# A two-layer diffusion backbone on one core: operand build in single splits, a deferred activation, and a down projection whose second half runs in reverse

## The chip, the cores and the metric

The kernel runs on one core of a Trainium2 chip. The core has TensorE (PE, matrix products; PEld is its loading of stationary operands), VectorE (DVE), ScalarE (ACT), GpSimd (POOL) and SyncE (SP, which here only issues DMAs). Each engine works through its own list of instructions in order. The metric is the device time of one execution in microseconds (us), lower is better.

## The reference

Two layers over 1024 latent tokens of width 1024 and, in the first layer, 256 context tokens. Layer 0 mixes tokens by a gated MLP in chunks of 128, layer 1 by windowed attention; each is followed by the same channel mixer, which is what most of the change touches:

```python
def conv_ffn(h, w_up, conv_w, conv_b, w_down):
    a, b = jnp.split(h @ w_up, 2, axis=-1)           # w_up (1024, 5632), so a and b have 2816 columns
    ap = jnp.pad(a, ((0, 0), (1, 1), (0, 0)))
    a = ap[:, :-2] * conv_w[0] + ap[:, 1:-1] * conv_w[1] + ap[:, 2:] * conv_w[2] + conv_b
    return (jax.nn.gelu(a) * b) @ w_down             # w_down (2816, 1024)
...
    for i in range(DEPTH):                           # 2
        mod_lat = silu(c) @ ada_w[i] + ada_b[i]      # six rows: shift, scale, gate, twice; the same for ctx
        h = modulate(rms_norm(x, norm_g[i, 0]), sh1, sc1)
        y, yc = chunk_mlp(...) if i == 0 else window_attention(...)
        x = x + g1 * rms_norm(y, norm_g[i, 1])
        h = modulate(rms_norm(x, norm_g[i, 2]), sh2, sc2)
        x = x + g2 * rms_norm(conv_ffn(h, f_w_up[i], ...), norm_g[i, 3])
```

## The kernel before

Every operand of a product is split into a high part (an ACT cast, `wh`, `ah` or `cmb`) and the rest (a DVE subtract, `wl`, `al` or `cmb`), so that each product is three matmuls (`mm3`). The weights come by SP's DMAs into three `raw` buffers, which all loads of the kernel share, and are split from there (`split_into`).

**Order.** The code is written as generators: `step` takes one piece of a side job (a weight's split, a column of the operand build) between products. A scheduler then orders each engine's list by its own estimates; the lists are fixed before the kernel runs. The lines that time belongs to are hidden behind one helper (L50), so the rows name tiles.

**Layer 0 up.** First 22 context blocks (`up_ctx`, 48 matmuls of 256 columns each, with weights of 128 columns of a and of b) with `combine(0)` and `combine(1)` as side jobs in 44 steps: they load the modulated tokens (`xT`) and build seven split operands (`COMBOS`, tiles `cmb`) for Strassen's scheme. Then 22 Strassen blocks (`up`), each 7 products of 12 matmuls of 512 columns; their weight sums t1 to t4 are built by `weights` while the block before runs. X, Y and Z are PSUM tiles (`psB`): the copy of b1 reads Y after the second product, and a PSUM tile must be read before a product overwrites it. `conv_gate` does the convolution (two DVE adds), gelu (ACT), the product with b (DVE) and the store to `actd`; it runs beside the next block's products.

**Layer 0 down.** Two halves of 512 output columns. Each loads all 22 activation blocks (`act_hl`, tiles `ah` and `al`) and the weights of its half, two blocks a load; eight PSUM banks (four in two `psA` tiles, four in `psB`) gather eight token tiles. The last blocks of a half run bank by bank, and `finish` reads each bank, by a square on ACT (`junk`) and a gated copy on DVE (`y`). As a side job the sums of the next layer's ada weights run on DVE (`dacc`, 32 loads: two sets of eight with two sums each, two sets with one).

**Layer 1** has the same without context: attention ends in an output product (`last_o`), then a few plain blocks beside `combine(0)`, 22 Strassen blocks (five of them half ones, `g1`, 256 columns), and the down projection. `flip` (transposes of a normed tile, with eight modulates from PSUM to SBUF) stands between mixers and channel mixers.

Of the kernel before, what the change touches and what calls it, by code (L numbers as in the profile page):

```python
# [10 lines left out]
F32 = mybir.dt.float32  # L11
# [4 lines left out]
P = 128  # L16
# [16 lines left out]
def hybrid_kernel(  # L33
# [151 lines left out]

    def ada_sums(l, m, streams, accs):
        for k in range(KD):
            raw = t_raw()
            Q.dma_start(raw, ada_w[l, k * P:(k + 1) * P, m * D:(m + 1) * D])
            for s, acc in zip(streams, accs):  # L190
                cc = ccols[:, 8 * s + k:8 * s + k + 1]
                if k == 0:
                    V.tensor_scalar(out=acc, in0=raw, scalar1=cc, scalar2=None, op0=ALU.mult)
                else:
                    V.scalar_tensor_tensor(out=acc, in0=raw, scalar=cc, in1=acc, op0=ALU.mult, op1=ALU.add)
            yield
# [91 lines left out]
    def flip(stage, t, xn, wide=False, mod=None):  # L288
        xt = t_row(shape=(P, KD, P))
        pw = psA((P, KD, P)) if wide else None  # L290
        pq = [pw[:, 4 * q:4 * q + 4, :] if wide else psB((P, 4, P)) for q in range(2)]
        for k in range(KD):
            T.transpose(out=pq[k // 4][:, k % 4, :], in_=xn[:, k * P:(k + 1) * P], identity=ident)
        for k in range(KD if mod else 0):
            gg, sh = (mod_cols(mod[0], m, 0 if t < 8 else 1)[:, k:k + 1] for m in (mod[1] + 1, mod[1]))
            S.activation(xt[:, k, :], pq[k // 4][:, k % 4, :], AF.Identity, bias=sh, scale=gg)
        for q in range(0 if mod else 2):
            S.copy(xt[:, 4 * q:4 * q + 4, :], pq[q])
        S.dma_start(xT[stage][:, :, t * P:(t + 1) * P], xt)
        return xt  # L300
# [631 lines left out]
    def weights(l, f, out, plain):  # L932
# [24 lines left out]
        t1, t3, t2, t4 = t13[:, 0:512], t13[:, 512:1024], t24[:, 0:512], t24[:, 512:1024]  # L957
        G.tensor_tensor(out=t1, in0=b12, in1=b11, op=ALU.subtract)
        V.tensor_sub(t2, b22, t1)
        G.tensor_tensor(out=t3, in0=b22, in1=b12, op=ALU.subtract)  # L960
        V.tensor_sub(t4, b21, t2)
        yield
        pair((b11, ("b11",)), (t2, ("t2",)))
        yield
# [7 lines left out]
    def lat_ffn(l, stage, n0, halos, gate, between, steady, ctx=None, after=None):  # L972
# [18 lines left out]
        def combine(g):  # L991
            for c in range(2):
# [12 lines left out]
                if ctx is not None:  # L1005
# [7 lines left out]
                    yield  # L1013
                put("a11", a11)
                put("a12", a12)
                if n0 and g == 0:
                    split_into([A21[c][:, z] for z in range(2)], a21)
                put("a22", a22)
                yield
                G.tensor_tensor(out=s1, in0=a21, in1=a22, op=ALU.add)  # L1020
                V.tensor_tensor(out=s2, in0=s1, in1=a11, op=ALU.subtract)
                put("s2", s2)
                G.tensor_tensor(out=s3, in0=a11, in1=a21, op=ALU.subtract)
                put("s1", s1)
                yield
                put("s3", s3)
                V.tensor_tensor(out=s4, in0=a12, in1=s2, op=ALU.subtract)
                put("s4", s4)
                yield
# [10 lines left out]
        def conv_gate(f, a, N, b, where):  # L1040
# [4 lines left out]
                                   op0=ALU.mult, op1=ALU.add)  # L1045
            S.activation(c, c, AF.Gelu_apprx_tanh)
            cv = c.rearrange("p (h n) -> p h n", n=256) if len(b.shape) == 3 else c
            V.tensor_tensor(out=cv, in0=cv, in1=b, op=ALU.mult)
            Q.dma_start(actd[f, :, where:where + N], c)

# [57 lines left out]
        def up(f, groups, nxt):  # L1108
# [31 lines left out]
            S.copy(b1, wide(Y[:, 0:n]))  # L1140
            V.tensor_tensor(out=b1, in0=b1, in1=wide(s1), op=ALU.add)
            product(Z, "s1", "t1", True)
            s5 = t_s()[:, 0:n]
# [42 lines left out]
        for (f, how), nxt in zip(jobs, jobs[1:] + [None]):  # L1186
# [7 lines left out]
            step(steady)  # L1194

        open_pool("down%d" % l)
        pool = stage_pool["pool"]
        ks = list(range(n0, NF)) + list(range(n0))
        ys, sums = {}, []
        if ctx is not None:  # L1200
            extra = chain(*[sums_of(pool, sums, 1, m, streams)
# [4 lines left out]
        def act_hl(k, own):  # L1206
            raw = t_raw()
            Q.dma_start(raw, actd[k, :, 0:SEQ])
            hl = [t_w("w" + z) if own else pool.tile([P, 1024], F32R, name=nm("a" + z), tag="a" + z, bufs=7)
                  for z in "hl"]  # L1210
# [9 lines left out]

        parts = {}
        for h in range(2):
            pair = [psA() for _ in range(2)]
            banks = [pair[i // 2][:, i % 2, :] for i in range(4)] + [psB() for _ in range(4)]
            ws, hls = {}, {}

            def step_(n, i):
                (ah, al), (wh, wl) = hls[n], ws[n]
                tk = slice(i * P, (i + 1) * P)
                mm3(banks[i], ah[:, tk], al[:, tk], wh, wl, n == 0, n == NF - 1)  # L1230

            def fetch(n):
                hls[n] = act_hl(ks[n], h == 0 and n < 2)
                if n % 2 == 0:
# [8 lines left out]

            nk = NF - (2, 6)[h]
            for n in range(nk):
# [31 lines left out]
    def sums_of(pool, sums, l, m, streams):  # L1277
        accs = [pool.tile([P, 1024], F32, name=nm("dacc"), tag="dacc%d%d" % (m, s), bufs=1) for s in streams]
        yield from ada_sums(l, m, streams, accs)
        sums.append((m, streams, accs))  # L1280
# [566 lines left out]
```

## Time and profile before

| | |
|---|---|
| median of 3 runs | 2988.23 us (2986.74 to 2988.72) |
| profiled execution | 2990.52 us, span 2988.7 us, mean granted clock 0.988 |
| busy: TensorE | 2851.6 us (95% of the span), weight loads 2411.1 |
| busy: DVE, ACT, POOL | 2023.8 (68%), 1380.9 (46%), 675.6 (23%) |
| DMA | 493.32 MB, mean 165 GB/s |

In the tables of stretches the granted clock is a mean over the stretch: TensorE's clock has two levels, 2.4 GHz (1.00) and 1.2 GHz (0.5). Waits are named by the engine and tile that waited, and what released it. The stages by time: gated MLP to 780, context blocks to about 925, Strassen blocks of layer 0 to 1381, its down projection to 1640, context down projection and attention to 2250, the start of layer 1's channel mixer to 2340, its Strassen blocks to 2735, its down projection to the end.

### The profile page before, as it was taken

What the parts mean: (1) busy time and instruction counts of PE and PEld (TensorE: products, weight loads), DVE (VectorE), ACT (ScalarE), POOL (GpSimd) and SP (SyncE); (2) the same over time, 40 slices, a digit from 0 to 9 for tenths busy, and PEclk for the clock granted to TensorE, in tenths of its full rate; (3) what the DMA queues carried; (4) which work ended last, traced back from release to release, by engine and by line L of the source; (5) the groups of instructions that cost most, each with busy time, mean ns of one, the idle gap of its engine ahead of it and who ended that gap; (6) DMA issues with size and microseconds to landing.
All of it is one profiled execution on the core that took longest, in us unless ns stands there. A gap on an engine that the chain in (4) does not pass through costs nothing. (4 is left out here: it accounts for less than half of the span.)

```text
span 2988.7 us, 40216 instructions
## 1 busy us (share of the span) xinstructions
PE 2851.6 (95%) x14834; PEld 2411.1 (81%) x14834; DVE 2023.8 (68%) x3008; ACT 1380.9 (46%) x2341; POOL 675.6 (23%) x1019
## 2 busy tenths in 40 slices
PE   7999999999889999999999999999998999999999
PEld 5799888998789777887778777788887878888887
DVE  6457674756586778777663659897776877776333
ACT  4332242422675444543333534787886444444331
POOL 1151120720311112220002114565453211110000
PEclk9999999999999999999999999999998999999999
DMA  8764355532675323445775875347576333235542
GB/s 265 231 182 140 124 192 181 170 97 71 201 216 157 108 92 113 160 158 177 229 233 178 267 257 173 105 150 238 170 243 211 103 121 103 82 95 174 189 148 99
DMA packets 403750, 493.32 MB, mean 165 GB/s; under 512 B 17633, under 2 KB 297057, under 8 KB 403553
## 3 DMA queue, kind: packets, MB, share of 16 engines
q1 hardware_dynamic: 347137, 427.56, 44.8%
q10 hardware_dynamic: 55264, 58.99, 5.7%
q0 software_dynamic: 1152, 4.19, 0.4%
q8 instruction: 117, 1.92, 0.3%
q14 instruction: 80, 0.66, 0.1%
HBM read 394.21 MB, written 96.47 MB: 164 GB/s over the span
## 5 line engine op out<-in xcount | busy, mean ns | idle before, releaser
L50 PE MATMUL psB<-cmb,wh 128*128 128x512 f32 (+2 forms) x2584 | 758.6, 378 | 18.7 <-ACT row L50 16.3
L50 ACT CAST wh<-raw 128x1024 fp32r<-128x1024 f32 (+1 forms) x388 | 345.9, 903 | 491.3 <-PE psB L50 202.9
L50 PEld LDWEIGHTS psB<-cmb,wh 128*128 128x128 f32 x2584 | 469.5, 188 | 124.6 <-ACT row L50 28.8
L50 DVE TENSOR_TENSOR wl<-raw,wh 128x1024 fp32r<-128x1024 f32 (+1 forms) x388 | 404.3, 1053 | 155.2 <-ACT wh L50 154.2
L50 PE MATMUL psB<-cmb,wl 128*128 128x512 f32 (+2 forms) x1292 | 486.4, 376 | 0.0
L50 PE MATMUL psB<-wh,big 128*128 128x512 f32 x864 | 288.7, 401 | 2.1 <-ACT big L50 1.3
L50 PEld LDWEIGHTS psB<-cmb,wl 128*128 128x128 f32 x1292 | 242.8, 188 | 48.2
L50 POOL TENSOR_SCALAR sm<-sm 128x1 f32<-128x1 f32 (+1 forms) x76 | 36.7, 482 | 882.4 <-ACT junk L50 329.8
L50 DVE TENSOR_TENSOR al<-raw,ah 128x1024 fp32r<-128x1024 f32 x84 | 102.8, 1225 | 176.8 <-ACT ah L50 176.7
L50 POOL TENSOR_TENSOR row<-raw,raw 128x512 f32<-128x512 f32 x44 | 72.4, 1646 | 641.1 <-DMA raw<-in_f_w_up_dram 533.5
L50 PE MATMUL psB<-wh,act 128*128 128x512 f32 x640 | 202.9, 395 | 1.6 <-DVE tmp L50 1.6
L50 ACT CAST ah<-raw 128x1024 fp32r<-128x1024 f32 x84 | 87.9, 1048 | 251.0 <-DMA raw<-actd 126.4
L50 PEld LDWEIGHTS psB<-wh,big 128*128 128x128 f32 x864 | 163.7, 190 | 41.7 <-ACT big L50 2.4
L50 PE MATMUL psA<-big,wh 128*128 128x320 f32 x1024 | 194.5, 312 | 2.8 <-ACT wh L50 1.7
L50 ACT CAST wh<-row 128x512 fp32r<-128x512 f32 (+1 forms) x132 | 100.9, 765 | 150.3 <-PE psB L50 66.3
L50 PE MATMUL psB<-wl,big 128*128 128x512 f32 x432 | 168.3, 399 | 0.0
L50 DVE SCALAR_TENSOR_TENSOR row<-row,cwcols,row 128x1024 f32<-128x1024 f32 (+2 forms) x142 | 146.6, 1034 | 31.7 <-issue 16.8
L50 PEld LDWEIGHTS psA<-big,wh 128*128 128x128 f32 x1024 | 160.8, 189 | 3.8 <-ACT wh L50 2.2
L50 POOL TENSOR_SCALAR row<-row,sm,sm 128x128 f32<-128x128 f32 x160 | 121.1, 771 | 148.6 <-DMA row<-vscr 147.9
L50 DVE TENSOR_TENSOR row<-raw,row 128x512 f32<-128x512 f32 (+2 forms) x101 | 117.5, 1163 | 46.9 <-POOL row L50 46.7
L50 PE MATMUL psA<-wh,ah 128*128 128x512 f32 x336 | 133.8, 401 | 14.2 <-ACT wh L50 7.7
L50 PE MATMUL psB<-row,wh 128*128 128x256 f32 x744 | 141.9, 292 | 5.4 <-ACT wh L50 5.2
(263 smaller groups left out, 6248.3 us busy)
## 6 DMA issues: line engine op xcount, KB each, us to landing
raw<-in_f_w_up_dram SPq DMA_DIRECT2D x142, 512.0 KB, 4.8
raw<-in_ada_w_dram SPq DMA_DIRECT2D x96, 512.0 KB, 4.6
raw<-actd SPq DMA_DIRECT2D x93, 512.0 KB, 4.0
raw<-in_a_w_in_dram SPq DMA_DIRECT2D x64, 512.0 KB, 4.7
wh<-woscr SPq DMA_DIRECT2D x48, 512.0 KB, 3.7
raw<-in_f_w_down_dram SPq DMA_DIRECT2D x88, 256.0 KB, 4.1
actd<-row SPq DMA_DIRECT2D x39, 512.0 KB, 2.6
raw<-in_a_w_out_dram SPq DMA_DIRECT2D x35, 512.0 KB, 3.4
```

Source lines behind the costliest of these rows:

```text
L50: ins = fn(*a, **kw)
```

## The change

Five edits. (a) `flip`: the odd ones of the eight modulates go from ACT to DVE. (b) `combine`: one split a step instead of three, s1 and s3 from POOL to DVE; eight or nine steps a column group instead of four or five. (c) `weights`: POOL's t1 and t3 in the first step; DVE's t2, its split, then t4 in the second (before, t2 and t4 in the first). (d) `conv_gate`: gelu, product with b and store are put off (`late`) and issued by `run_late` in the next block, behind the second product's b1 add; half blocks (N < 512) and context blocks do them at once. (e) `down`: the loads of the ada sums have two buffers of their own (`araw`), the second half takes the 22 blocks in reverse and keeps the last five splits of the first (`KEEP`), so it loads 17 blocks of activations instead of 22; in layer 0 the splits have 6 buffers instead of 7, and the last 5 blocks (before 6) run bank by bank.

```diff
     def ada_sums(l, m, streams, accs, space=None):
         for k in range(KD):
-            raw = t_raw()
+            raw = (space or t_raw)()
...
         for k in range(KD if mod else 0):
             gg, sh = (mod_cols(mod[0], m, 0 if t < 8 else 1)[:, k:k + 1] for m in (mod[1] + 1, mod[1]))
-            S.activation(xt[:, k, :], pq[k // 4][:, k % 4, :], AF.Identity, bias=sh, scale=gg)
+            if k % 2:
+                V.tensor_scalar(out=xt[:, k, :], in0=pq[k // 4][:, k % 4, :], scalar1=gg, scalar2=sh,
+                                op0=ALU.mult, op1=ALU.add)
+            else:
+                S.activation(xt[:, k, :], pq[k // 4][:, k % 4, :], AF.Identity, bias=sh, scale=gg)
...
         G.tensor_tensor(out=t1, in0=b12, in1=b11, op=ALU.subtract)
+        G.tensor_tensor(out=t3, in0=b22, in1=b12, op=ALU.subtract)
+        yield
         V.tensor_sub(t2, b22, t1)
-        G.tensor_tensor(out=t3, in0=b22, in1=b12, op=ALU.subtract)
+        pair((b11, ("b11",)), (t2, ("t2",)))
         V.tensor_sub(t4, b21, t2)
-        yield
-        pair((b11, ("b11",)), (t2, ("t2",)))
         yield
...
                 put("a11", a11)
+                yield
                 put("a12", a12)
                 if n0 and g == 0:
                     split_into([A21[c][:, z] for z in range(2)], a21)
+                yield
                 put("a22", a22)
+                V.tensor_tensor(out=s1, in0=a21, in1=a22, op=ALU.add)
                 yield
-                G.tensor_tensor(out=s1, in0=a21, in1=a22, op=ALU.add)
+                put("s1", s1)
                 V.tensor_tensor(out=s2, in0=s1, in1=a11, op=ALU.subtract)
+                yield
                 put("s2", s2)
-                G.tensor_tensor(out=s3, in0=a11, in1=a21, op=ALU.subtract)
-                put("s1", s1)
+                V.tensor_tensor(out=s3, in0=a11, in1=a21, op=ALU.subtract)
                 yield
                 put("s3", s3)
                 V.tensor_tensor(out=s4, in0=a12, in1=s2, op=ALU.subtract)
+                yield
                 put("s4", s4)
...
-            S.activation(c, c, AF.Gelu_apprx_tanh)
-            cv = c.rearrange("p (h n) -> p h n", n=256) if len(b.shape) == 3 else c
-            V.tensor_tensor(out=cv, in0=cv, in1=b, op=ALU.mult)
-            Q.dma_start(actd[f, :, where:where + N], c)
+
+            def rest():
+                S.activation(c, c, AF.Gelu_apprx_tanh)
+                cv = c.rearrange("p (h n) -> p h n", n=256) if len(b.shape) == 3 else c
+                V.tensor_tensor(out=cv, in0=cv, in1=b, op=ALU.mult)
+                Q.dma_start(actd[f, :, where:where + N], c)
+
+            late.append(rest)
+            if len(b.shape) == 3 or N < 512:
+                run_late()
...
             V.tensor_tensor(out=b1, in0=b1, in1=wide(s1), op=ALU.add)
+            run_late()
             product(Z, "s1", "t1", True)
...
         if ctx is not None:
             extra = chain(*[sums_of(pool, sums, 1, m, streams)
                             for m, streams in ((0, (0, 1)), (1, (0, 1)), (3, (0,)), (4, (0,)))])
...
-            hl = [t_w("w" + z) if own else pool.tile([P, 1024], F32R, name=nm("a" + z), tag="a" + z, bufs=7)
+            hl = [t_w("w" + z) if own else pool.tile([P, 1024], F32R, name=nm("a" + z), tag="a" + z, bufs=7 if ctx is None else 6)
...
             def fetch(n):
-                hls[n] = act_hl(ks[n], h == 0 and n < 2)
+                if h == 0 or n >= KEEP:
+                    hls[ks[n]] = act_hl(ks[n], h == 0 and n < 2)
...
-            nk = NF - (2, 6)[h]
+            nk = NF - (2, 6 if ctx is None else 5)[h]
+            if h == 1:
+                ks.reverse()
...
-        yield from ada_sums(l, m, streams, accs)
+        yield from ada_sums(l, m, streams, accs,
+                            lambda: pool.tile([P, 1024], F32, name=nm("araw"), tag="araw", bufs=2))
```

How the lists move at three places (before first, then after; `...` leaves rows out).

DVE in a Strassen block of layer 0. `wl_1480` is the last split of the running block's weights, the SCALAR_TENSOR_TENSOR rows on `row_1481` are the two convolution adds, `row_1489` holds t2 and then t4, `gate` is an ada sum, `row_1491` is b.

```order
L50 TENSOR_TENSOR wl_1480_9633<-row_1468_9511,wh_1479_9632 128x512
L50 SCALAR_TENSOR_TENSOR row_1481_9636<-row_1474_9591,cwcols0_688,row_1481_9636 128x1024
L50 TENSOR_TENSOR row_1489_9655<-raw_1487_9651,row_1488_9654 128x512
L50 SCALAR_TENSOR_TENSOR row_1481_9636<-row_1474_9591,cwcols0_688,row_1481_9636 128x1024
L50 TENSOR_TENSOR row_1489_9655<-raw_1486_9650,row_1489_9655 128x512
L50 SCALAR_TENSOR_TENSOR gate_1354_8777<-raw_1503_9787,ccols_90,gate_1354_8777 128x1024
L50 TENSOR_TENSOR row_1481_9636<-row_1481_9636,row_1470_9542 128x1024
L50 TENSOR_TENSOR row_1491_9686<-row_1491_9686,s_1490_9672 128x2x256
L50 TENSOR_TENSOR wl_1494_9705<-raw_1486_9650,wh_1493_9704 128x512
```

```order
L50 TENSOR_TENSOR wl_1480_9633<-row_1468_9508,wh_1479_9632 128x512
L50 SCALAR_TENSOR_TENSOR row_1481_9636<-row_1474_9591,cwcols0_688,row_1481_9636 128x1024 x2
L50 SCALAR_TENSOR_TENSOR gate_1354_8774<-raw_1503_9784,ccols_90,gate_1354_8774 128x1024
L50 TENSOR_TENSOR row_1481_9636<-row_1481_9636,row_1470_9537 128x1024
L50 TENSOR_TENSOR row_1491_9681<-row_1491_9681,s_1490_9667 128x2x256
L50 TENSOR_TENSOR row_1489_9652<-raw_1487_9648,row_1488_9651 128x512
L50 TENSOR_TENSOR wl_1494_9704<-raw_1486_9647,wh_1493_9703 128x512
L50 TENSOR_TENSOR row_1489_9652<-raw_1486_9647,row_1489_9652 128x512
L50 TENSOR_TENSOR wl_1494_9704<-row_1489_9652,wh_1493_9703 128x512
```

t2 stood between the two adds and t4 behind them; now both adds stand together, and t2 comes behind the product with b and the b1 add, beside the splits of b11 and t2.

ACT at the start of the context blocks. `wh_1091` and `wh_1095` are the casts of the next block's weights, `row_1050` and `row_1041` the flips' modulates, `row_1053`, `row_1055` and `row_972` (each with an `sm`) the squares of norms, `row_1088` a context block's copy.

```order
L50 CAST wh_1048_6782<-raw_1038_6724 128x1024
L50 ACTIVATE row_1050_6786<-psB_1051_6787,modc_83 128x128 x4
L50 ACTIVATE row_1050_6786<-psB_1052_6788,modc_83 128x128 x4
L50 ACTIVATE row_1055_6811,sm_1056_6812<-row_972_6368 128x1024
...
L50 COPY row_1088_6877<-psB_1086_6851 128x256
L50 CAST wh_1091_6885<-raw_1089_6881 128x1024
L50 ACTIVATE row_1053_6806,sm_1093_6889<-row_1044_6755 128x1024
...
L50 ACTIVATE row_972_6368,sm_1094_6895<-row_1054_6809 128x1024
...
L50 CAST wh_1095_6925<-raw_1090_6882 128x1024
```

```order
L50 CAST wh_1048_6782<-raw_1038_6724 128x1024
L50 ACTIVATE row_1041_6731<-psB_1042_6732,modc_83 128x128
L50 ACTIVATE row_1041_6731<-psB_1043_6733,modc_83 128x128
L50 CAST wh_1091_6885<-raw_1089_6881 128x1024
L50 ACTIVATE row_1050_6786<-psB_1051_6787,modc_83 128x128
L50 ACTIVATE row_1041_6731<-psB_1042_6732,modc_83 128x128
L50 ACTIVATE row_1041_6731<-psB_1043_6733,modc_83 128x128
L50 CAST wh_1095_6925<-raw_1090_6882 128x1024
...
L50 ACTIVATE row_1050_6786<-psB_1051_6787,modc_83 128x128
L50 ACTIVATE row_1050_6786<-psB_1052_6788,modc_83 128x128 x2
L50 ACTIVATE row_1055_6811,sm_1056_6812<-row_972_6368 128x1024
...
L50 COPY row_1088_6877<-psB_1086_6851 128x256
L50 ACTIVATE row_1053_6806,sm_1093_6889<-row_1044_6755 128x1024
```

Both casts stood behind the flip and among the squares; now they stand ahead of all three squares and between single modulates, and the flips have half as many modulates here.

DVE at the turn of the halves in layer 0's down projection. `al` is a split of activations, `wl` of weights, `dacc` an ada sum, `y` the read of a bank.

```order
L50 SCALAR_TENSOR_TENSOR dacc_1895_12362<-raw_1970_12728,ccols_90,dacc_1895_12362 128x1024
L50 TENSOR_TENSOR al_1973_12734<-raw_1971_12731,ah_1972_12733 128x1024
L50 SCALAR_TENSOR_TENSOR dacc_1895_12362<-raw_1974_12761,ccols_90,dacc_1895_12362 128x1024
L50 SCALAR_TENSOR_TENSOR dacc_1895_12362<-raw_1975_12764,ccols_90,dacc_1895_12362 128x1024
L50 TENSOR_TENSOR al_1978_12770<-raw_1976_12767,ah_1977_12769 128x1024
L50 TENSOR_TENSOR wl_1981_12777<-raw_1979_12773,wh_1980_12776 128x1024
L50 SCALAR_TENSOR_TENSOR dacc_1895_12362<-raw_1982_12804,ccols_90,dacc_1895_12362 128x1024
L50 TENSOR_TENSOR y_1935_12596<-psA_1806_11819,gate_1354_8777 128x512
L50 TENSOR_TENSOR al_1985_12810<-raw_1983_12807,ah_1984_12809 128x1024
L50 SCALAR_TENSOR_TENSOR dacc_1895_12362<-raw_1986_12837,ccols_90,dacc_1895_12362 128x1024
L50 TENSOR_TENSOR y_1938_12608<-psA_1806_11819,gate_1354_8777 128x512
L50 TENSOR_TENSOR y_1941_12620<-psA_1807_11820,gate_1354_8777 128x512
```

```order
L50 SCALAR_TENSOR_TENSOR dacc_1895_12362<-araw_1974_12813,ccols_90,dacc_1895_12362 128x1024
L50 SCALAR_TENSOR_TENSOR dacc_1895_12362<-araw_1978_12847,ccols_90,dacc_1895_12362 128x1024
L50 TENSOR_TENSOR al_1981_12853<-raw_1979_12850,ah_1980_12852 128x1024
L50 TENSOR_SCALAR dacc_1982_12880<-araw_1983_12881,ccols_90 128x1024
L50 SCALAR_TENSOR_TENSOR dacc_1982_12880<-araw_1984_12884,ccols_90,dacc_1982_12880 128x1024
L50 TENSOR_TENSOR wl_1972_12759<-raw_1970_12755,wh_1971_12758 128x1024
L50 SCALAR_TENSOR_TENSOR dacc_1982_12880<-araw_1991_12924,ccols_90,dacc_1982_12880 128x1024
L50 SCALAR_TENSOR_TENSOR dacc_1982_12880<-araw_1995_12957,ccols_90,dacc_1982_12880 128x1024
L50 SCALAR_TENSOR_TENSOR dacc_1982_12880<-araw_2002_12997,ccols_90,dacc_1982_12880 128x1024
L50 TENSOR_TENSOR wl_1977_12820<-raw_1975_12816,wh_1976_12819 128x1024
L50 TENSOR_TENSOR y_1935_12596<-psA_1806_11819,gate_1354_8774 128x512
L50 SCALAR_TENSOR_TENSOR dacc_1982_12880<-araw_2006_13030,ccols_90,dacc_1982_12880 128x1024
```

The first three `y` stood behind and between splits of the second half's activations; now seven ada sums (five of the last set, `dacc_1982`) and two splits of weights stand ahead of the first, and of activations only `al_1981`.

## Rows read from the trace of the kernel before

**Rows 1.** the page: busy us, share of the span and instructions of each engine

```profile
PE 2851.6 (95%) x14834; PEld 2411.1 (81%) x14834; DVE 2023.8 (68%) x3008; ACT 1380.9 (46%) x2341; POOL 675.6 (23%) x1019
```

**Rows 2.** stretches; us, busy us of PE, PEld, DVE, ACT, POOL, clock, DMA, GB/s

```profile
750.00:800.00 50.00, 44.34 (x236) 37.88 (x235) 31.00 (x32) 30.74 (x61) 21.32 (x29) 0.93 0.63 200
800.00:850.00 50.00, 41.03 (x301) 39.04 (x300) 34.97 (x48) 38.18 (x69) 7.06 (x16) 0.93 0.70 209
850.00:905.00 55.00, 50.24 (x393) 49.49 (x392) 44.49 (x62) 37.60 (x64) 7.14 (x24) 0.94 0.74 217
930.00:1340.00 410.00, 402.36 (x1762) 324.21 (x1761) 311.99 (x362) 189.51 (x279) 76.88 (x90) 1.00 0.37 122
1340.00:1500.00 160.00, 149.94 (x628) 117.86 (x627) 106.80 (x100) 53.32 (x59) 3.29 (x6) 0.99 0.63 204
1500.00:1600.00 100.00, 93.78 (x393) 75.15 (x393) 55.78 (x50) 33.54 (x44) 1.96 (x8) 0.97 0.69 223
2250.00:2300.00 50.00, 42.75 (x251) 36.80 (x250) 37.40 (x47) 34.08 (x64) 15.33 (x20) 0.90 0.65 203
2340.00:2735.00 395.00, 384.78 (x1847) 316.45 (x1846) 289.41 (x361) 180.68 (x284) 67.28 (x87) 1.00 0.32 100
```

**Rows 3.** waits, 764 to 920; engine, line, what for: total us, times, longest us

```profile
PE psB L50 <- DVE wl L50: 14.0, 10, 2.9
DVE wl L50 <- ACT wh L50: 26.8, 18, 5.6
```

**Rows 4.** TensorE in time, first context block; start, us, operation [idle before <- releaser]

```profile
793.04 0.58 PE L50 MATMUL psB<-row,wl 128*128 128x256 f32 x1 [2.88 <-DVE wl L50]
```

**Rows 5.** ACT in time, in the same stretch

```profile
782.77 2.89 ACT L50 ACTIVATE row<-psB,modc 128x128 f32<-128x128 f32 x8
```

**Rows 6.** operand build: DVE and TensorE in time

```profile
812.99 0.41 DVE L50 TENSOR_TENSOR row<-row,psB 128x256 f32<-128x256 f32 x1
817.06 3.00 DVE L50 TENSOR_TENSOR cmb<-row,cmb 128x512 fp32r<-128x512 f32 x3
841.18 0.39 PE L50 MATMUL psB<-row,wl 128*128 128x256 f32 x1 [2.81 <-DVE wl L50]
```

**Rows 7.** the Strassen block at 1000: POOL, DVE, ACT and TensorE in time

```profile
1003.10 1.55 POOL L50 TENSOR_TENSOR row<-raw,raw 128x512 f32<-128x512 f32 x1 [17.69 <-DMA raw<-in_f_w_up_dram]
1004.68 1.77 DVE L50 TENSOR_TENSOR row<-raw,row 128x512 f32<-128x512 f32 x1 [1.19 <-POOL row L50]
1006.37 1.27 DVE L50 SCALAR_TENSOR_TENSOR row<-row,cwcols,row 128x1024 f32<-128x1024 f32 x1
1007.67 1.06 ACT L50 ACTIVATE row<-row 128x1024 f32<-128x1024 f32 x1 [4.22 <-DVE row L50]
1009.25 0.73 PE L50 MATMUL psB<-cmb,wh 128*128 128x512 f32 x2 [0.83 <-ACT row L50]
```

**Rows 8.** waits of TensorE, 930 to 1340, then 2340 to 2735

```profile
PE psB L50 <- ACT row L50: 7.2, 9, 0.8
PE psB L50 <- ACT row L50: 8.2, 11, 1.1
```

**Rows 9.** the block at 1188: POOL, DVE and TensorE in time

```profile
1190.14 2.28 POOL L50 TENSOR_TENSOR row<-raw 128x512 f32<-128x512 f32 x1
1188.94 2.32 DVE L50 SCALAR_TENSOR_TENSOR row<-row,cwcols,row 128x1024 f32<-128x1024 f32 x1
1192.88 0.73 PE L50 MATMUL psB<-cmb,wh 128*128 128x512 f32 x2
```

**Rows 10.** 1340 to 1600: a wait, and DMA issues with us to landing

```profile
ACT ah L50 <- DMA raw<-actd: 106.2, 33, 7.2
raw<-in_ada_w_dram SPq DMA_DIRECT2D x32, 512.0 KB, 4.6
```

**Rows 11.** the turn of the halves: TensorE in time

```profile
1516.70 0.80 PE L50 MATMUL psA<-wh,ah 128*128 128x512 f32 x1 [6.22 <-DVE y L50]
```

**Rows 12.** start of layer 1, 2230 to 2345: a wait of TensorE

```profile
PE psA L50 <- ACT wh L50: 4.5, 1, 4.5
```

More of the change, by code (lines that the diff above doesn't have):

```diff
@@ L184, in finish_cols, with ada_sums @@
                                    op0=ALU.add, op1=ALU.mult)
-    def ada_sums(l, m, streams, accs):
+    def ada_sums(l, m, streams, accs, space=None):
         for k in range(KD):
-            raw = t_raw()
+            raw = (space or t_raw)()
             Q.dma_start(raw, ada_w[l, k * P:(k + 1) * P, m * D:(m + 1) * D])
@@ L1045, in conv_gate, with run_late @@
                                    op0=ALU.mult, op1=ALU.add)
-            S.activation(c, c, AF.Gelu_apprx_tanh)
-            cv = c.rearrange("p (h n) -> p h n", n=256) if len(b.shape) == 3 else c
-            V.tensor_tensor(out=cv, in0=cv, in1=b, op=ALU.mult)
-            Q.dma_start(actd[f, :, where:where + N], c)
+            def rest():
[6 more added lines that the diff above has]
+                run_late()
+        late = []
+        def run_late():
+            while late:
+                late.pop(0)()
         def next_weights(nxt):
@@ L1194, in lat_ffn @@
             step(steady)
+        run_late()
         open_pool("down%d" % l)
@@ L1199, in lat_ffn @@
         ys, sums = {}, []
+        KEEP = 5
         if ctx is not None:
@@ L1219, in finish @@
             return gated(p, gate(t)[:, hs], ys[t][:, hs], part, junk)
-        parts = {}
+        parts, hls = {}, {}
         for h in range(2):
@@ L1224, in lat_ffn @@
             banks = [pair[i // 2][:, i % 2, :] for i in range(4)] + [psB() for _ in range(4)]
-            ws, hls = {}, {}
+            ws = {}
             def step_(n, i):
-                (ah, al), (wh, wl) = hls[n], ws[n]
+                (ah, al), (wh, wl) = hls[ks[n]], ws[n]
                 tk = slice(i * P, (i + 1) * P)
```

## The prediction, before the changed kernel ran

> **What bounds the kernel now.** I read the page's busy table first: TensorE is busy 2851.6 us, 95% [rows 1]. No other engine is near that, so only time in which TensorE stands still or runs at its lower clock can be won. Next the table by stages [rows 2]. Idle time is the stretch less its PE time; the granted clock gives the rest: a mean of 0.93 over 50 us is 7 us at the lower level (1.2 instead of 2.4 GHz), which does 3.5 us less work.
> - 750 to 905 (context blocks of layer 0's up projection, operand build beside them): 155 less 135.6 is 19.4 idle, the clock some 10 more: 30.
> - 930 to 1340 (Strassen blocks, layer 0): 7.6 idle.
> - 1340 to 1600 (down projection, layer 0): 10.1 and 6.2 idle, clock 0.99 and 0.97 some 4: 20.
> - 2250 to 2300 (start of layer 1's mixer): 7.3 idle, clock 0.90 some 5: 12.
> - 2340 to 2735 (Strassen blocks, layer 1): 10.2 idle.
>
> Layer 1's down projection has no wait of TensorE in the view of waits, so its five kept splits win nothing there. Last, for each stage, the waits of TensorE, and the rows in order of time around them.
>
> **Context blocks and operand build.** TensorE waits ten times for `wl` of VectorE (DVE), 14.0 us, and DVE waits 18 times, 26.8 us, for the `wh` cast of ScalarE (ACT) ahead of it [rows 3]: ACT is late, or DVE behind it. The first block stands 2.88 us for `wl` at 793.04 [rows 4], since ACT has flips and the squares of norms ahead of its casts; a flip's eight modulates are 2.89 us [rows 5]. In the new order the casts of block 1 stand ahead of those squares, between single modulates, and a flip leaves ACT 1.44 us. What a 128x128 modulate from PSUM costs DVE isn't in the trace: at least nothing, where DVE waits for ACT anyway; at most 0.41, the 128x256 add from PSUM [rows 6]; four cost up to 1.6. I take 0.4 each, the nearest row; the 26.8 us of waits hide most. The build: now a step puts several splits in a row, as three `cmb` subtracts in 3.00 us at 817.06, and TensorE waits up to 2.81 for `wl` (841.18) [rows 6]. After, a step holds one split; 36 steps fill 44 places, so the build runs to about block 18 of 22. The sums s1 and s3 come to DVE: 4 x 2 at up to 1.00 each, what one of the three subtracts takes, is 8 us, on a DVE that is 70 and 81% busy in 800 to 905 [rows 2]. Bounds: all 30 is too much, because the weights' own casts and subtracts stay; a loss of 8 is the sums uncovered. I take 15, half: the casts' order mends the first blocks, the short steps the long waits, and the many short waits stay.
>
> **Strassen blocks.** In the block at 1000, POOL's t1 starts at 1003.10, when the weights land; DVE's t2 waits for t1 (1.19), takes 1.77 and stands ahead of the second convolution add (1006.37, 1.27); ACT's gelu waits 4.22 for that add; the copy of b1 stands behind gelu, and TensorE waits 0.83 for the copy [rows 7]. There are nine such waits, 7.2 us, in layer 0, and eleven, 8.2, in layer 1 [rows 8]. In the order of after, gelu still stands ahead of the copy on ACT, so the deferral alone moves nothing in these blocks; what moves is t2 on DVE, behind both adds. The second add can then start near 1003.5 instead of 1006.4, and it meets POOL's t1 and t3. What that costs is in the trace: at 1188.94 an add beside t1 and t3 took 2.32 instead of 1.27, and t3 2.28 instead of 1.29; in that block TensorE goes on at 1192.88 without a wait, with gelu and copy in the same order [rows 9]. For the block at 1000: t1 ends at 1004.65, the add 1.2 later at 1005.85, gelu at 1006.9, which is 1.8 us ahead of now, for 0.83 of wait. I take 7 of 7.2 and 8 of 8.2: the wait goes whole or, if the add is held longer than 1 us more, in part. t2 and its split come up to 4 us later on DVE, and are read by the next block's products, some 10 us on: covered.
> The Trainium skill (SBUF — State Buffer, Who interferes with whom) says that a DVE instruction with two SBUF inputs and a GpSimd instruction that reads SBUF exclude each other for the whole of the one that began. The trace agrees: 2.32 for 1.27. If POOL kept the pair for t1 and t3 in a row, the add would end at 1007.1 and about half of the waits would stay, 8 us less gain; the row at 1188.94, where t3 is the one that waits, speaks against it.
>
> **Down projection, layer 0.** Three raw buffers serve per block of 24 matmuls (5.5 us at 402.36 / 1762 [rows 2]) one load of activations, half a load of weights and 1.25 of the ada sums, 2.75 in all. A load lands about 4.6 us after issue [rows 10], and is freed by a cast (1.06) and a subtract (1.27), or one or two sums of 1.27 (pieces of 1024 columns, as in [rows 7]): 7 us. 2.75 x 7 / 3 = 6.4 us of loads per 5.5 us of matmuls, and ACT waits 106.2 us for activations [rows 10]. With two buffers for ada alone, the others need 1.5 x 7 / 3 = 3.5: ahead of TensorE. At the turn of the halves TensorE stands 6.22 us for DVE's `y` [rows 11]: the reads that drain the banks stand between splits that wait for activations. After, the eight squares stand together, and the second half starts with five blocks (28 us) that load weights alone. All of it is 20. The least is a loss, by the ada loads: 31 of 32 now stand ahead of the third `y` on DVE (before 23), on two buffers. A load with two sums needs (4.6 + 2.6) / 2 = 3.6, one with one 2.95: 16 x 3.6 + 15 x 2.95 = 102 us, in a half of 528 matmuls that takes 121 at best and now, with the 20, about 141. So it holds, with 0.6 us a load to spare for SP, which issues in order. I take 14.
>
> **Start of layer 1.** TensorE stands 4.5 us for `wh` [rows 12]; that cast comes earlier now. But two flips now stand right behind the first block's first product on TensorE, where the norm of the mixer's last tiles may not be done. A new wait there isn't in the trace; it lies between nothing and what the stage now loses, 12. I take 7 won and 4 given back: 3. In attention only the flips change: 0, plus or minus 3.
>
> **Sum.** 15 + 7 + 8 + 14 + 3 = 47 from the profiled execution's 2990.5: 2943.5. That execution is 2.3 us over the median: 2941.
>
> **Rivals.**
> - The fetches stay the bound: DVE, with sums and modulates added, keeps the `wl` waits in the context blocks (gain 5), and ada loads take over 4 us each, so `y` waits behind them (gain 2): 5 + 15 + 2 = 22, 2966. For it: DVE's 81%; against it: DVE itself waits 26.8 us for ACT.
> - The change doesn't do what it says in the Strassen blocks: gelu keeps its place on ACT, and if t1 and t3 together with the ada sum hold the second add, the 0.83 stays: 15 + 14 + 3 = 32, 2956. Against it: the block at 1188.
> - Much more: nearly all of 30, 20 and 12 goes: 26 + 15 + 19 + 9 = 69, 2919.
> - Slower: the ada loads run one at a time, because SP issues in order and a load that waits for its buffer holds the next behind it. 16 x 7.2 + 15 x 5.9 = 204 us for a half that now takes 141: +63 against 33 from the other parts, so 3018. The part loses from 4.5 us a load (141 / 31), the whole from 5.6. For it: 31 loads instead of 23 ahead of `y`, and SP's order; against it: two buffers let one land while the other is summed.
>
> **How the numbers follow.** Likeliest (0.57): 2941, own range 2931 to 2953. Fetches 0.16, Strassen blocks unchanged 0.12, much more 0.09, slower 0.06. Range 2918 to 2968: it leaves out the slower case and the outer ends. A measurement of this kernel tells 0.2% (6 us) from nothing: the slower case's 0.06 and the worst edge of the fetches' 0.02 make slower 0.05 and same 0.03, the rest faster 0.92.
>
> **What would show it.** Right: blocks of the Strassen stages without a wait of psB for ACT's row, each about 0.8 us shorter; fewer and shorter waits for `wl` in the context blocks and a granted clock near 1.00; at the turn of the halves no wait for `y` over 1 us, and ACT's 106 us for activations down; a new wait of TensorE in the flips at layer 1's start. Wrong: DVE's `dacc` waiting for ada loads ahead of `y`, an add beside POOL of well over 2.4 us, or a wait that has moved into attention.

## The result and the profile after

The changed kernel takes 2944.8 us (median of 4 runs, 2941.13 to 2947.62) against 2988.38 before (4 runs beside it); the ratio is 0.9855, 95% interval 0.9837 to 0.9872. The forecast was 2941. The profiled execution took 2941.13, the fastest of the four, so its sum comes out 5.8 us better against the execution profiled before (2990.52) than the medians do. The page's span and TensorE's busy time after:

```profile
span 2939.4 us, 40162 instructions
PE 2830.1 (96%) x14834; PEld 2406.6 (82%) x14834; DVE 2033.0 (69%) x3066; ACT 1353.9 (46%) x2279; POOL 683.9 (23%) x1003
```

TensorE runs the same 14834 matmuls in both kernels, so a stage can be cut at the same matmul in both traces, wherever it lies in time. The table of stretches for such cuts, of the kernel before (cut at round times, up to 0.2 us beside the matmul; columns as in [rows 2]; context blocks, Strassen blocks of layer 0, first half of its down projection, start of layer 1, Strassen blocks of layer 1):

```profile
780.00:925.00 145.00, 125.61 (x955) 121.86 (x954) 105.95 (x141) 101.40 (x176) 22.70 (x60) 0.93 0.74 219
925.00:1381.60 456.60, 448.12 (x1979) 362.02 (x1978) 340.80 (x395) 210.39 (x308) 80.30 (x98) 1.00 0.37 121
1381.60:1527.00 145.40, 129.96 (x532) 101.35 (x531) 98.60 (x86) 45.62 (x53) 1.39 (x5) 0.96 0.74 239
2250.00:2340.00 90.00, 82.65 (x584) 76.42 (x583) 67.77 (x83) 59.98 (x117) 28.64 (x33) 0.94 0.58 180
2340.00:2735.00 395.00, 384.78 (x1847) 316.45 (x1846) 289.41 (x361) 180.68 (x284) 67.28 (x87) 1.00 0.32 100
```

and of the changed kernel between the same matmuls:

```profile
779.48:906.35 126.87, 119.30 (x955) 117.09 (x954) 102.41 (x154) 90.52 (x155) 9.10 (x46) 0.96 0.80 237
906.35:1351.96 445.61, 444.64 (x1980) 363.37 (x1978) 351.74 (x403) 213.03 (x314) 89.46 (x102) 1.00 0.39 127
1351.96:1484.35 132.39, 125.30 (x532) 100.75 (x530) 103.64 (x93) 42.24 (x51) 1.54 (x7) 0.97 0.84 286
2203.78:2300.66 96.88, 82.53 (x584) 78.02 (x583) 72.23 (x112) 55.99 (x104) 21.64 (x25) 0.93 0.57 174
2300.66:2685.47 384.81, 382.28 (x1847) 317.04 (x1846) 294.50 (x357) 180.93 (x283) 76.92 (x86) 1.00 0.32 102
```

The second column is the length of each stage. The differences, good to 0.2 us, beside the forecast's terms:

| stage | forecast | measured |
|---|---|---|
| context blocks | -15 | -18.1 |
| Strassen blocks, layer 0 | -7 | -11.0 |
| down projection, layer 0 (first half) | -14 | -13.0 |
| start of layer 1 | -3 | +6.9 |
| Strassen blocks, layer 1 | -8 | -10.2 |
| all else | 0 | about -4 |
| sum | -47 | -49.4 |

One term has the wrong sign, and the down projection reached its size by another way than was forecast. Each stage stands here as one execution of each kernel has it; how far executions differ is said ahead of the experiments.

**Strassen blocks.** One block of the changed kernel, on POOL, DVE, ACT and TensorE:

```profile
984.05 1.29 POOL L50 TENSOR_TENSOR row<-raw,raw 128x512 f32<-128x512 f32 x1 [16.09 <-DVE row L50]
985.30 2.28 POOL L50 TENSOR_TENSOR row<-raw 128x512 f32<-128x512 f32 x1
982.67 3.75 DVE L50 SCALAR_TENSOR_TENSOR row<-row,cwcols,row 128x1024 f32<-128x1024 f32 x2 [0.82 <-issue]
986.46 1.06 ACT L50 ACTIVATE row<-row 128x1024 f32<-128x1024 f32 x1 [2.54 <-DVE row L50]
987.42 0.57 ACT L50 COPY row<-psB 128x512 f32<-128x512 f32 x1
988.02 0.63 PE L50 MATMUL psB<-cmb,wh 128*128 128x512 f32 x2
```

The two adds follow each other: 3.75 us where two alone take 2.55, because the second meets POOL's t1. Gelu starts 3.8 us after the adds began, with no t2 ahead of the second as in [rows 7], and TensorE goes on without a wait. The Trainium skill (SBUF — State Buffer, Who interferes with whom), weighed in the prediction, fits here: add and t1 exclude each other. Of t3 and the add it is again t3 that waits (2.28 us), as in [rows 9]. Over the whole stages, no wait of psB for ACT's row is left in layer 0, and in layer 1

```profile
PE psB L50 <- ACT row L50: 0.4, 1, 0.4
```

**The turn of the halves.** DVE and TensorE there, after:

```profile
1457.17 1.23 DVE L50 TENSOR_TENSOR al<-raw,ah 128x1024 fp32r<-128x1024 f32 x1 [3.49 <-ACT ah L50]
1463.98 1.28 DVE L50 SCALAR_TENSOR_TENSOR dacc<-araw,ccols,dacc 128x1024 f32<-128x1024 f32 x1 [1.35 <-DMA araw<-in_ada_w_dram]
1469.81 2.61 DVE L50 SCALAR_TENSOR_TENSOR dacc<-araw,ccols,dacc 128x1024 f32<-128x1024 f32 x2 [4.54 <-DMA araw<-in_ada_w_dram]
1472.33 1.22 DVE L50 TENSOR_TENSOR wl<-raw,wh 128x1024 fp32r<-128x1024 f32 x1
1473.46 0.69 DVE L50 TENSOR_TENSOR y<-psA,gate 128x512 f32<-128x512 f32 x1
1474.20 0.79 PE L50 MATMUL psA<-wh,ah 128*128 128x512 f32 x1 [7.09 <-DVE y L50]
```

The wait of [rows 11] is still there and longer, 7.09 instead of 6.22, with another cause: `y` stands behind ada sums that wait 4.54 us for their load. What was won is the first half before it: the waits of ACT for activations from 1340 to 1600 went from 106.2 us [rows 10] to

```profile
ACT ah L50 <- DMA raw<-actd: 43.3, 16, 11.0
```

and TensorE waits for nothing but `y` there.

**The start of layer 1.** DVE, POOL and TensorE, after:

```profile
2233.97 3.49 DVE L50 TENSOR_TENSOR wl<-raw,wh 128x1024 fp32r<-128x1024 f32 x3
2233.71 4.42 POOL L50 TENSOR_SCALAR sm<-sm 128x1 f32<-128x1 f32 x1 [4.28 <-ACT row L50]
2238.86 1.12 POOL L50 TENSOR_SCALAR row<-row,rstT 128x1024 f32<-128x1024 f32 x1
2240.03 1.97 PE L50 MATMUL psA<-ident,row 128*128 128x128 f32 x8 [9.64 <-POOL row L50]
```

TensorE stands 9.64 us at the first flip, whose tile POOL finishes only then; 4.2 of them are POOL's small instruction at 2233.71, which takes 0.19 us elsewhere (more in the last section). The wait for `wh` of [rows 12] is gone.

### The profile page after: what moved, and what is told of

Read it like the earlier page. It is cut to its first block, busy times and chain, and to the rows that moved or that the text cites. A ratio compares the mean times of both kernels' runs of the same rounds, so it can differ in the third digit from the quotient of the medians.

```text
span 2939.4 us, 40162 instructions
## 1 busy us (share of the span) xinstructions
PE 2830.1 (96%) x14834; PEld 2406.6 (82%) x14834; DVE 2033.0 (69%) x3066; ACT 1353.9 (46%) x2279; POOL 683.9 (23%) x1003
## 5 line engine op out<-in xcount | busy, mean ns | idle before, releaser
L50 DVE TENSOR_TENSOR al<-raw,ah 128x1024 fp32r<-128x1024 f32 x74 | 90.5, 1224 | 170.9 <-ACT ah L50 170.5
L50 DVE SCALAR_TENSOR_TENSOR row<-row,cwcols,row 128x1024 f32<-128x1024 f32 (+2 forms) x142 | 160.9, 1133 | 38.4 <-issue 17.8
L50 ACT CAST ah<-raw 128x1024 fp32r<-128x1024 f32 x74 | 77.4, 1048 | 226.8 <-PE psB L50 158.8
L50 PEld LDWEIGHTS psB<-wh,act 128*128 128x128 f32 x640 | 120.1, 188 | 30.1 <-issue 1.0
```

The costliest lines, as they stand in the source:

```text
L50: ins = fn(*a, **kw)
```

## The experiments

Each kernel differs from the changed one by the edit shown. Ratios are to the kernel before on the same chip; stage times are between the same matmuls as above. The context stage takes 126.87 to 132.57 us in the ten executions that have the changed kernel's list there (126.87 is the changed kernel's own), so a difference of that size in it says nothing. The first half of layer 0's down projection takes 132.39 to 136.35 us in the six executions with the changed list there (132.39 again the changed kernel's own). All of that spread is the wait for `y`, 7.1 to 10.3 us: up to the turn the half takes 114.8 us in all eleven executions with ada's own buffers, and 128.1 in both without (before, and one experiment). The start of layer 1 takes 95.44 to 97.23 us in the seven executions with the changed list there.

**The weights' sums back in the old order.**

```diff
+        V.tensor_sub(t2, b22, t1)
         G.tensor_tensor(out=t3, in0=b22, in1=b12, op=ALU.subtract)
+        V.tensor_sub(t4, b21, t2)
         yield
-        V.tensor_sub(t2, b22, t1)
         pair((b11, ("b11",)), (t2, ("t2",)))
-        V.tensor_sub(t4, b21, t2)
```

> The changed kernel with the weights' sums in the old order (t2 and t4 on DVE in the first step, between the two convolution adds); the deferred activation and all else stay. Theory: t2's place on DVE is what the Strassen blocks won by, so TensorE waits about 0.83 us for ACT's row again in nine blocks of layer 0 and in about eleven of layer 1, and the kernel takes about 18 us more than the changed one: near 2963. Rival: the deferred gelu is what pays; then it stays within 4 us of the changed kernel's 2945.

2968.53 us, ratio 0.993 (0.9912 to 0.9948). The Strassen stages are 10.9 and 10.5 us longer than in the changed kernel, as long as before. TensorE's waits there, layer 0 and then layer 1 (columns as in [rows 3]):

```profile
PE psB L50 <- ACT row L50: 8.1, 10, 0.9
PE psB L50 <- ACT row L50: 8.8, 10, 1.3
```

These are much the waits of [rows 8]. t2's place on DVE is what these stages won by, and the deferral, which this kernel keeps, wins nothing without it.

**The activation at once.**

```diff
-            if len(b.shape) == 3 or N < 512:
+            if True:
                 run_late()
```

> The changed kernel with the activation issued at once, as before; t2 stays moved. Theory: in the blocks with ada sums the lists are the same, in the later ones gelu goes ahead of the copy of b1 again, which costs at most 0.25 us in each of some 25 blocks: 2945 to 2951. Rival (the deferral pays): 0.83 us come back in some 20 blocks: near 2963.

2952.19 us, ratio 0.9877 (0.9857 to 0.9897). The Strassen stages are 1.5 and 0.9 us longer than in the changed kernel, with these waits:

```profile
PE psB L50 <- ACT row L50: 1.1, 2, 0.6
PE psB L50 <- ACT row L50: 1.1, 3, 0.5
```

So beside t2's move the deferral is worth some 2 us in them, not nothing and not 18 (executions with the changed kernel's lists there differ by up to 1 us and 0.4). The rest of the 7 us between the medians lies in stages that the edit doesn't touch.

**The old build in layer 1 alone** (the steps of `combine` as before where there is no context).

```diff
+                if ctx is None:
+                    put("a11", a11)
+                    put("a12", a12)
...
+                    put("a22", a22)
+                    yield
+                    G.tensor_tensor(out=s1, in0=a21, in1=a22, op=ALU.add)
...
+                    continue
                 put("a11", a11)
                 yield
```

> The changed kernel with the old operand build (three splits a step, s1 and s3 on POOL) in layer 1 alone. Theory: the 9.64 us for which TensorE stands at layer 1's flips come from the flips' new place behind the first block's first product, and that place comes from the build in single splits; with the old build the flips stand behind two further products, that wait goes, the old waits for wh and wl (4.5 and 2.1 us) come back in part: 5 to 8 us less than the changed kernel, near 2938. Rival: the chain of the norm on POOL makes the wait wherever the flips stand; then the old waits are added and it takes 2945 to 2951.

2944.29 us, ratio 0.9844 (0.9822 to 0.9866): by the medians no change. The stage itself answers: 88.35 us instead of 96.88, and its waits of TensorE are

```profile
PE psA L50 <- DVE wl L50: 3.6, 3, 2.0
PE psA L50 <- ACT wh L50: 2.3, 3, 0.9
```

with none at the flips. The profiled execution (2944.97) lost 12.4 us against the changed kernel's in stages that the edit leaves alone: 4.5 in the context stage (131.35), 3.0 between layer 0's down projection and layer 1, 2.0 at the turn of the halves, the rest spread. The theory holds for the stage: the flips stand behind 144 matmuls of the blocks instead of 52, and POOL is done with their tiles 4.8 us ahead of TensorE. The forecast for the whole missed; that the gain reaches it is seen with the kernel with both edits below.

**The reads of the banks first.** The ada sums that the second half's steps trace are queued on DVE behind the last of the eight reads.

```diff
...
                     parts[i] = finish(i, 0, banks[i], EPS)
+                    y_read[i] = last["V"].ins
                     continue
...
-                if h or n < 14:
-                    step(extra, 1 + (n % 4 == 1))
+                if h and ctx is not None:
+                    with tc.issue_after(y_read[7]):
+                        step(extra, 1 + (n % 4 == 1))
+                elif n < 14:
+                    step(extra, 1 + (n % 4 == 1))
```

> The changed kernel with the ada sums of the second half's steps queued on DVE behind the eight reads of the banks (y) at the turn of layer 0's down projection; same work. Theory: the 7.1 us for which TensorE stands there are the ada loads ahead of y on DVE; they go, and the stretch at the lower clock behind them: 7 to 10 us less, near 2936. Rival: the reads wait for ACT's squares or the second half's loads anyway, or the ada loads moved into the second half delay its activations by as much: 2943 to 2950.

2937.7 us, ratio 0.9831 (0.9812 to 0.9851). The stage takes

```profile
1354.98:1478.42 123.44, 123.44 (x531) 99.47 (x530) 87.38 (x79) 42.23 (x51) 1.33 (x7) 1.00 0.76 256
```

9.0 us less than in the changed kernel, and less than in any execution with its list. TensorE is busy in all of it, at the full clock; the second half is not longer (113.26 us, 113.27 in the changed kernel). The ada sums ahead of `y` were the whole wait.

**Three buffers for ada** (`bufs=3` for `araw`).

> The changed kernel with three buffers for the ada loads instead of two. The list keeps eight ada sums between the last split of the first half and the first read of a bank. Theory: the read waits because the ada loads come at the rate of two buffers (about 3 us each); with three the rate is 2 us, and the 7.1 us of TensorE's wait shrink to 0 to 4: 2938 to 2944. Rival: SP's order or the shared transfers set the rate, not the buffers; the wait stays above 6 us, 2944 to 2949.

2945.1 us, ratio 0.9861 (0.9843 to 0.9879). The stage takes 129.73 us, 2.7 less than the shortest with the changed list, and the wait is half as long or less:

```profile
PE psA L50 <- DVE y L50: 3.4, 1, 3.4
```

The wait halves with a third buffer, as the theory has it; the median, a little above the forecast, is too coarse for 2.7 us.

**Ada loads in the shared buffers again** (`ada_sums` is called without buffers of its own, so each load takes a `t_raw()`).

> The changed kernel with the ada sums of layer 0's down projection loaded into the three shared raw buffers again; reverse order and kept splits stay. Theory: buffers were what the first half waited for, so ACT's waits for activations and TensorE's gaps in the first half come back, 8 to 12 us between 1381 and 1527, and y is waited for as well: 2953 to 2958. Rival: the kept splits made the gain; then it stays within 3 us of 2945.

2956.81 us, ratio 0.9901 (0.9875 to 0.9927). The stage takes 144.54 us, 8 to 12 more than with the changed list, all of what it had won. TensorE's longest waits:

```profile
PE psA L50 <- ACT wh L50: 7.5, 6, 3.2
PE psA L50 <- DVE y L50: 4.9, 1, 4.9
```

Up to the turn the half takes 128.1 us again, as before. The buffers made the gain (with the order that the lists take by them); reverse order and kept splits, still in this kernel, don't make it alone.

**Without reverse order and kept splits.**

```diff
-                if h == 0 or n >= KEEP:
+                if True:
                     hls[ks[n]] = act_hl(ks[n], h == 0 and n < 2)
...
-            if h == 1:
-                ks.reverse()
```

> The changed kernel without the reverse order and the kept splits: the second half loads and splits all 22 blocks again; ada's own buffers stay. On DVE four splits of the second half's activations and seven ada sums now stand ahead of the first read of a bank. Theory: the first half's gain is the buffers' and stays, the wait at the turn stays or grows (7 to 12 us), the rest of the second half is unchanged: 0 to 5 us more than the changed kernel between 1381 and 1527, 2945 to 2950. Rival: the kept splits carry the turn, without them the second half starves: 8 us and more.

2946.88 us, ratio 0.9868 (0.9848 to 0.9888); the stage 133.91 us with a wait of 7.9 for `y`, both inside the spread of the changed list: no difference can be told here. **The same edit on the kernel with both improvements** (the one further below):

> The fastest kernel so far (old build in layer 1, reads first) without the reverse order and the kept splits. Theory: with the reads first on DVE, the kept splits win little, since the second half's loads can run ahead in six buffers: 0 to 3 us more than its 2925. Rival: the second half starts without activations, a wait of 5 us or more at the turn: 2931 to 2937.

2929.07 us, ratio 0.9809 (0.9787 to 0.9831); the stage 125.56 us with a wait of 1.9 for `y`, 2.1 more than the 123.43 and 123.44 us of the two executions with reads first and kept splits, which have no such wait. There the kept splits are worth about 2 us.

**All modulates on ACT.**

```diff
-            if k % 2:
-                V.tensor_scalar(out=xt[:, k, :], in0=pq[k // 4][:, k % 4, :], scalar1=gg, scalar2=sh,
-                                op0=ALU.mult, op1=ALU.add)
-            else:
-                S.activation(xt[:, k, :], pq[k // 4][:, k % 4, :], AF.Identity, bias=sh, scale=gg)
+            S.activation(xt[:, k, :], pq[k // 4][:, k % 4, :], AF.Identity, bias=sh, scale=gg)
```

> The changed kernel with all eight modulates of a flip on ACT, as before. The list of ACT at the start of the context blocks is then that of before (both casts behind the flip and among the squares). Theory: the casts' place is worth 5 to 8 us of the 18 won between 780 and 925, and the rest, the build, stays: 2951 near the median. Rival: the split flip pays nothing there, the build does all: 2945 to 2947.

2946.0 us, ratio 0.9867 (0.9844 to 0.9891). The context stage takes 128.97 us, within the spread of the changed kernel's list. ACT and TensorE in the first block:

```profile
782.83 1.06 ACT L50 ACTIVATE row<-row 128x1024 bf16<-128x1024 f32 x1
784.28 1.05 ACT L50 CAST wh<-raw 128x1024 fp32r<-128x1024 f32 x1
788.77 0.38 PE L50 MATMUL psB<-row,wl 128*128 128x256 f32 x1 [2.88 <-DVE wl L50]
```

and in the kernel before:

```profile
787.11 1.06 ACT L50 ACTIVATE row<-row 128x1024 bf16<-128x1024 f32 x1 [1.45 <-DMA xT<-row]
789.66 0.50 PE L50 MATMUL psB<-row,wh 128*128 128x256 f32 x2 [2.61 <-ACT wh L50]
```

The list is that of before, the 2.88 us for `wl` of [rows 4] are there to the hundredth, but the wait of 2.61 for the cast ahead of it is not, since here the square did not wait for a transfer as it did before at 787.11; the stretch at the lower clock behind is some 3 us long instead of 5. The theory falls: the casts' new place pays nothing that can be seen. The changed list has waits of its own there, since TensorE now stands for the flips' modulates that were mixed with the casts (in the changed kernel):

```profile
781.33 0.65 PE L50 MATMUL psB<-row,wh 128*128 128x256 f32 x2 [1.46 <-ACT row L50]
783.30 0.58 PE L50 MATMUL psB<-row,wh 128*128 128x256 f32 x1 [1.32 <-DVE row L50]
```

This edit also shortens the start of layer 1, which its theory didn't speak of: 92.50 us, 3 to 5 less than with the changed list. The flips stand 23 matmuls later there, and TensorE's wait at them is

```profile
PE psA L50 <- POOL row L50: 6.2, 1, 6.2
```

So the split flip has a part in the new wait there, beside the build. What the modulates cost DVE was bounded by 0 and 0.41 us; the groups of the changed kernel between 750 and 800 have (us busy, mean ns)

```profile
L50 DVE TENSOR_SCALAR row<-psB,modc 128x128 f32<-128x128 f32 x12 | 4.4, 405 | 0.9 <-ACT row L50 0.7
```

which is the upper bound.

**The old build in both layers.**

> The changed kernel with the old operand build in both layers. The start of the context blocks keeps the new list. Theory: in layer 0 the long waits for wl in the middle of the context blocks come back, 8 to 12 us between 780 and 925, and layer 1's start is 8.5 shorter, as with the old build there alone: 2945 to 2949. Rival: the build costs nothing in layer 0 since the first block was all: 2936.

2949.2 us, ratio 0.9876 (0.9853 to 0.9899). The context stage takes 137.50 us, 5 to 11 more than in the kernels with the new build, and layer 1's start 91.53 instead of 96.88: 5.3 us where the theory had 8.5 (the four executions with the old build there take 86.89 to 91.53). The long waits for `wl` in mid-build are back, as at 841.18 in [rows 6]; in time:

```profile
832.71 0.58 PE L50 MATMUL psB<-row,wl 128*128 128x256 f32 x1 [2.83 <-DVE wl L50]
```

and in the view of waits, over the stage, where the changed kernel has 3.4 us in four:

```profile
PE psB L50 <- DVE wl L50: 11.5, 8, 3.1
```

The build is worth 5 to 11 of the 12 to 18 us that the stage won; whether by the shorter steps or by s1 and s3 on DVE wasn't tried apart. The other 7.5 us (144.96 before, 137.50 here) lie nearly all in the stage's first 228 matmuls: 43.61 us before, 36.76 here, 38.45 with all modulates on ACT, 36.14 in the changed kernel. They stay won with either edit undone, so these runs give them to none, and of the kernel before there is one profiled execution alone.

**Both improvements** (old build in layer 1, reads first).

> The changed kernel with the old operand build in layer 1 alone and the ada sums of the second half queued behind the eight reads of the banks. Theory: the two waits are in different stages and don't meet, so the two gains add, 8.5 and 9 us off the changed kernel: 2927, between 2922 and 2932. Rival: what is won in one place is waited for in the next (attention, whose lists move with the ada columns): 2933 to 2938.

2925.17 us, ratio 0.9798 (0.9777 to 0.9819): 2% under before, and the fastest kernel of this study. The five stages:

```profile
778.83:905.71 126.88, 118.61 (x955) 115.64 (x953) 102.44 (x154) 90.47 (x155) 9.13 (x46) 0.97 0.81 238
905.71:1351.60 445.89, 444.65 (x1979) 363.47 (x1979) 351.67 (x402) 212.61 (x315) 89.33 (x102) 1.00 0.39 127
1351.60:1475.03 123.43, 123.43 (x532) 99.50 (x531) 87.31 (x79) 42.26 (x51) 1.32 (x7) 1.00 0.76 256
2197.43:2284.32 86.89, 82.08 (x584) 75.91 (x583) 71.41 (x99) 54.94 (x101) 27.33 (x32) 0.96 0.59 183
2284.32:2669.11 384.79, 382.20 (x1847) 317.05 (x1846) 297.65 (x361) 181.61 (x284) 78.04 (x87) 1.00 0.33 103
```

The third and fourth are 9.0 and 10.0 us under the changed kernel's, and the others equal: in the stages the two gains add.

## Why the prediction was right, and where not

The sum is nearer than its terms. The 10 us by which the start of layer 1 missed are covered by three stages that won 2 to 4 us more than was forecast and by 4 us in stages put at 0; that is luck, and so is the profiled execution's 2941.13, 3.7 us under its median.

- **Strassen blocks: right, mechanism and place.** The change of order of t2 does it, and the deferral next to nothing. The term was sized by the idle time alone (0.83 a block); with the restart behind each wait, which the working gave to neither stage, it is about 1.0 (at the wait of [rows 7] the matmuls start 1.22 us apart instead of 0.23), smaller waits of other blocks go too, and 11.0 and 10.2 us came instead of 7 and 8. That the deferral "alone moves nothing" holds: with it and t2 in the old place the stages are as long as before. Beside t2's move it is worth 2 us that the working didn't have, in the later blocks, where gelu and the copy of b1 do change places on ACT.
- **Down projection: size right, turn wrong.** The step that failed is "So it holds, with 0.6 us a load to spare". It spread 31 loads over the whole half. The list puts the last seven between the last split of the half and the first `y`, and the sums there come 3.2 us apart on the average of the last five, unevenly (those at 1463.98 and 1469.81 lie 5.8 apart). So the rival's mechanism, `y` behind ada loads, which the prediction also lists as a sign of being wrong, was at work in this one place: 7.09 us of wait, and 9.0 with the lower clock behind it. The gain came from the first half before the turn, 13.3 us (128.1 to 114.8) where the wait for activations had been, and the stage would have won 22 without the new wait. By the executions of the same list it won 9 to 13. The kept splits, which the step gave the five blocks of the second half's start, are worth about 2.
- **Start of layer 1: wrong sign.** The step named the place and the wait, and sized it at 4 between 0 and 12, "7 won and 4 given back". The wait measured 9.64. It comes from the flips' place behind the first block's first product, which comes from the build's edit: with the old build in layer 1 it is gone and the stage 5 to 10 us shorter. Two parts the working didn't have: the split flip moves the flips forward as well (without it the wait is 6.2), and POOL's small instruction, held for 4.42 us, lies in the wait.
- **Context blocks: right in size, half right in cause.** The build is worth 5 to 11 us, and the whole stage won 12 to 18, by the executions of the same list. The step that failed is "the casts' order mends the first blocks": undone, it costs nothing, and the new order has waits of its own at the start. 7.5 us of the stage are not settled. The granted clock went from 0.93 to 0.96, not near 1.00.
- **All else** was put at 0 and came to some -4 in one execution. Most of it lies between layer 0's second half and layer 1, where executions of nearly equal lists differ by as much (719 to 724 us).

## What to carry to other kernels

When a side job gets buffers of its own, its instructions run further ahead in the engine's list; look at what they now stand in front of at the next turn, and compare the rate of its loads there with the time the next reader has, not with the whole stage. An operation that is ready late and blocks an in-order queue (a transpose behind a norm) must stand behind work that covers it: here 144 matmuls covered it and 52 didn't. An edit far from it can move it, by the lists that the scheduler makes, so look where such operations went after every edit. And stages cut at the same matmul in two traces tell what each edit did when the medians of whole runs can't (those of the kernel before range from 2984.5 to 2988.9); but set each against the spread of that stage in executions with the same list, or a wait that varies by 3 us looks like an effect.

## What the runs showed of the hardware that was not expected

A POOL instruction on 128x1 elements, 0.19 us elsewhere in the same chain, took 4.42 us at 2233.71 while DVE ran instructions with two SBUF inputs without a gap, and ended at 2238.13, 0.05 us after the last of them. In the kernel with the reads first the same instruction took 4.02 us, in the one with all modulates on ACT 4.81 us, and in both it also ended 0.05 us behind DVE's run. It stood in the chain that TensorE waited for at layer 1's flips. At 985.30 POOL's t3 waited for one add alone (2.28 us instead of 1.29). What decides between the two wasn't tried.
